# Down products of the feed-forward layers as seven products in two sweeps, with weight sums made by accumulating transfers

## The chip, the cores and the metric

One core of one Trainium2 chip runs the whole program. The metric is the device time of one execution in microseconds, the median of several runs.

## The reference

A stack of three layers over x of 512 tokens by 1024, all float32. Two layers (layer 0 and layer 1) have attention, a memory attention over 256 further tokens, and a gated feed-forward part; the last layer has two other attentions and a feed-forward part with squared relu. The change touches the last product of each feed-forward part:

```python
# layers 0 and 1, D_FF = 2816
h = rms_norm(x, norm_ffn_pre[i])
gu = jnp.einsum('bsd,df->bsf', h, w_gu[i])
f = jnp.einsum('bsf,fd->bsd', jax.nn.silu(gu[..., :D_FF]) * gu[..., D_FF:], w_down[i])
x = x + rms_norm(f, norm_ffn_post[i])
# last layer, D_FF_2 = 4096
a = relu(rmsnorm(x, norm_mlp_g) @ w_mlp_in) ** 2
x = x + a @ w_mlp_out
return rmsnorm(x, norm_final_g)
```

The last three lines are the reference's, in short. In the down product a 512 x 2816 (or 4096) matrix of activations meets a weight matrix of 2816 (4096) x 1024.

## The kernel before

Every float32 product is made of three float32r products: each factor is split into a high and a low part, and `mm3` (L262 to L264) issues high·high, high·low and low·high into one PSUM bank. The high part of a weight half chunk is an ACT cast (L250), the low part a DVE subtraction (L252); both stand in `split`. `loader` walks the list `order` and streams weight chunks of 512 KB (128 x 1024) with SP transfers (L236).

The order of the instructions is set when the program is built: tasks written as generators yield operations, and a list scheduler with priorities, tile pools ("slot", 37 tiles of 4 KB per partition, with a cap per use in `CAPS`) and a pool of 8 PSUM banks puts them one after another on each engine. On the chip each engine then runs its list in order and waits on semaphores.

A feed-forward part is `ffn` (L1354). Its up and gate products are already in a seven-product form: `seven` (matmuls L1224 to L1226 into `z`, column sums of weights on DVE at L1164, splits at L1090 and L1092). They leave activations in tiles `act`, features on partitions, two feature tiles of 128 x 512 tokens in each slot.

The down product is plain. A task in `ffn` splits every activation tile into `jit` tiles (ACT L1400, DVE L1402), once for each half of the output's 1024 columns. `out_product` (L491) takes the two halves in turn: four banks `acc`, one for each block of 128 tokens, over all 22 (32) feature tiles, three 128x512 matmuls each. So there are 2 x 4 x 22 x 3 = 528 matmuls in layers 0 and 1 each, and 768 in the last. In the second half of the columns the last 8 feature tiles are held back and done one token block after another, so that the blocks finish one by one.

The end of a block is `first_half` (L552: times the gain, or L545: into x) and `second_half` (L578 times the gain, L567 in the last layer; sum of squares on ACT at L406; `rsqrt` in eight small DVE steps L381 to L396; x plus the scaled product at L587). Then `to_norm` norms x for the next layer (L451), transposes it on PE (L465, tiles `ht`) and splits it (ACT L476, DVE L478) into the tiles `h` that the next projection reads.

In layer 0 the task of the second layer's memory keys and values is spawned from `post`, at the start of the down product: 96 matmuls 128x256 (`b<-mh,w` and `b<-w,mh`, through L262 to L264), with their own norm and transposes, then L642 and L644. In the order PE has most of them among the transposes of the tail.

Of the kernel before, what the change touches and what calls it, by code (L numbers as in the profile page):

```python
# [11 lines left out]
F32R = mybir.dt.float32r  # L12
# [7 lines left out]
S = 512  # L20
# [9 lines left out]
CAPS = dict(raw=2, w=8, q=2, k=4, p=5, pT=3, h=3, gain=2, f0=2, tmp=3, act=16, jit=8, bias=4, y=2,  # L30
# [125 lines left out]
class Chunk:  # L156


    def __init__(self, name, i):
        self.name, self.i = name, i  # L160
        self.half = [Fut(), Fut()]
        self.raw, self.unread = None, 2


class Builder:
# [9 lines left out]
    def setup(self):  # L175
# [22 lines left out]
        self.order = []  # L198
        self.hready = None
# [25 lines left out]
    def chunk(self, name, i):  # L225
        c = Chunk(name, i)
        self.order.append(c)
        return c

    def loader(self):  # L230
        nc, sc = self.nc, self.S
        for n, c in enumerate(self.order):
            r = yield ("get", "slot", "raw", 1)
            raw = self.tile_slot((P, 2, 512), name="raw")
            fin = yield ("op", "SP", r, 0.06)
            nc.sync.dma_start(raw.rearrange("p a b -> p (a b)"), self.ap[c.name][c.i])  # L236
            busy = self.arrival(fin, 512)
# [7 lines left out]
    def split(self, c, h, raw, ready, rel):  # L245
        nc, sc = self.nc, self.S
        r = yield ("get", "slot", "w", 1)
# [847 lines left out]
    def token_sums(self, out):  # L1095
# [14 lines left out]
        def put(name, src, t, dst=None):  # L1110
            if dst is None:
# [3 lines left out]
                self.held += 2  # L1115
# [64 lines left out]
    def seven(self, cs, gated, acts, slots, j0):  # L1180
# [11 lines left out]
        self.h_read, self.held = Fut(), 0  # L1192
# [10 lines left out]
        def product(n, name, banks, first=False, last=False, ready=0.0, waits=(None, None)):  # L1203
# [7 lines left out]
            for e in range(2):  # L1211
# [17 lines left out]
                if name in after:  # L1229
                    after[name](state[n], e, t)  # L1230
            return ts
# [75 lines left out]
        for n in range(nd):  # L1307
# [7 lines left out]
            s["rt"] = yield ("get", "slot", "tmp", 2)  # L1315
            s["ta"], s["tb"] = [self.tile_slot((P, 2, S), name="tmp") for _ in range(2)]
# [23 lines left out]
        sc.put("slot", sc.t["PE"], None, self.held)  # L1340
# [13 lines left out]
    def ffn(self, ci, co, nf, gated, post, nxt):  # L1354
# [35 lines left out]
        yield from self.seven(ci[4:], gated, acts, slots, 4 // per)  # L1390

        jit = {(k, half): Fut() for half in range(2) for k in range(nf)}

        def splitter(half):
            for k in range(nf):
                r = yield ("get", "slot", "jit", 1)
                w = self.tile_slot((P, 2, S), F32R, name="jit")
                f = yield ("fut", acts[k])
                t = yield ("op", "ACT", max(f.t, r), act(S, False))
                nc.scalar.copy(w[:, 0], f.val)  # L1400
                t = yield ("op", "DVE", t, dve(S))
                nc.vector.tensor_tensor(w[:, 1], f.val, _f(w[:, 0]), ALU.subtract)  # L1402
                reads[k // 2] += 1
# [600 lines left out]
```

## Time and profile before

| what | value |
|---|---|
| median of 3 runs | 1942.0 us (1941.7 to 1944.85) |
| profiled execution | 1943.43 us, span 1941.3 us, mean granted clock 0.995 |
| PE busy | 1903.5 us, 12282 instructions |
| DVE busy | 1351.7 us |
| ACT busy | 1012.2 us |
| POOL busy | 83.5 us |
| down products of layer 0 | 443.9 to 566.8 us, tail to 586.6 |
| down products of layer 1 | 1041.3 to 1162.2 us, tail to 1178.5 |
| down products of the last layer | 1759.3 to 1933.4 us, end at 1941.3 |

The span is the time from the first to the last recorded instruction of the profiled execution; its own time, 2.1 us longer, takes in what lies around. Busy time is a sum over instructions, so it says how full an engine is on average; what an engine waits for in one stretch is read from the rows of that stretch. Matmuls are pipelined: the time shown for one is longer than the distance from its start to that of the next.

### The profile page before, as it was taken

What the parts mean: (1) busy time and instruction counts of PE and PEld (TensorE: products, weight loads), DVE (VectorE), ACT (ScalarE), POOL (GpSimd) and SP (SyncE); (2) the same over time, 40 slices, a digit from 0 to 9 for tenths busy, and PEclk for the clock granted to TensorE, in tenths of its full rate; (3) what the DMA queues carried; (4) which work ended last, traced back from release to release, by engine and by line L of the source; (5) the groups of instructions that cost most, each with busy time, mean ns of one, the idle gap of its engine ahead of it and who ended that gap; (6) DMA issues with size and microseconds to landing.
All of it is one profiled execution on the core that took longest, in us unless ns stands there. A gap on an engine that the chain in (4) does not pass through costs nothing.

```text
span 1941.3 us, 31689 instructions
## 1 busy us (share of the span) xinstructions
PE 1903.5 (98%) x12282; PEld 1656.7 (85%) x12282; DVE 1351.7 (70%) x2767; ACT 1012.2 (52%) x2229; POOL 83.5 (4%) x145
## 2 busy tenths in 40 slices
PE   7999999999999999999999999999999999999998
PEld 6877899998887777899999889777778889998886
DVE  7576898887666665798888556337752659996562
ACT  6686455556545554455556535445553335555460
POOL 2000000000003221000000000000000000000000
PEclk9999999999999999999999999999999999999999
DMA  8113232332332333223323332231232322332331
GB/s 289 36 64 120 77 109 88 108 119 106 121 110 80 96 97 112 88 77 104 115 87 109 111 116 73 93 98 55 82 114 77 122 73 77 99 105 103 109 108 44
DMA packets 54149, 192.66 MB, mean 99 GB/s; under 512 B 6954, under 2 KB 6974, under 8 KB 54000
## 3 DMA queue, kind: packets, MB, share of 16 engines
q1 hardware_dynamic: 47664, 171.46, 26.3%
q0 software_dynamic: 6336, 19.19, 3.5%
q8 instruction: 96, 1.57, 0.3%
q14 instruction: 53, 0.43, 0.1%
HBM read 180.83 MB, written 3.17 MB: 95 GB/s over the span
## 4 chain that ended last, share of the span: by engine, by line
PE 94%; DVE 4%; ACT 1%; issue 1%; DMA 0%; SPq 0%; DVEq 0%; ACTq 0%
PE b L262 10%; PE acc L262 10%; PE acc L264 9%; PE acc L263 9%; PE b L264 9%; PE b L263 9%; PE z L1226 9%; PE z L1224 9%; PE z L1225 9%; PE o L709 3%; PE tr L682 3%; PE s L658 2%; PE s L661 2%; PE ht L465 1%; DVE w L1092 1%
## 5 line engine op out<-in xcount | busy, mean ns | idle before, releaser
L252 DVE TENSOR_TENSOR w<-raw,w 128x512 fp32r<-128x512 f32 x408 | 269.7, 688 | 133.9 <-ACT w L250 131.8
L1092 DVE TENSOR_TENSOR w<-raw,w 128x512 fp32r<-128x512 f32 x378 | 246.7, 688 | 36.8 <-ACT w L1090 34.6
L262 PE MATMUL b<-h,w 128*128 128x512 f32 (+1 forms) x736 | 269.4, 366 | 1.7 <-ACT h L476 1.7
L250 ACT CAST w<-raw 128x512 fp32r<-128x512 f32 x408 | 239.6, 620 | 32.5 <-DVE jit L1402 11.0
L263 PE MATMUL b<-h,w 128*128 128x512 f32 (+1 forms) x736 | 254.3, 346 | 1.4 <-DVE h L478 1.4
L264 PE MATMUL b<-h,w 128*128 128x512 f32 (+1 forms) x736 | 254.8, 346 | 0.0
L1090 ACT CAST w<-raw 128x512 fp32r<-128x512 f32 x378 | 223.6, 621 | 51.3 <-DVE raw L1164 50.7
L1226 PE MATMUL z<-h,w 128*128 128x256 f32 x864 | 242.4, 281 | 5.6 <-DVE w L1092 5.6
L1224 PE MATMUL z<-h,w 128*128 128x256 f32 x864 | 242.7, 281 | 1.0 <-ACT w L1090 1.0
L1225 PE MATMUL z<-h,w 128*128 128x256 f32 x864 | 241.6, 280 | 0.0
L262 PE MATMUL acc<-w,jit 128*128 128x512 f32 x608 | 237.4, 390 | 0.0
L264 PE MATMUL acc<-w,jit 128*128 128x512 f32 x608 | 236.7, 389 | 0.0
L263 PE MATMUL acc<-w,jit 128*128 128x512 f32 x608 | 236.5, 389 | 0.0
L1226 PE MATMUL z<-so,w 128*128 128x256 f32 x648 | 183.7, 284 | 3.0 <-DVE w L1092 2.9
L1224 PE MATMUL z<-so,w 128*128 128x256 f32 x648 | 183.5, 283 | 0.0
L1225 PE MATMUL z<-so,w 128*128 128x256 f32 x648 | 183.3, 283 | 0.0
L1226 PEld LDWEIGHTS z<-h,w 128*128 128x128 f32 x864 | 163.0, 189 | 6.7 <-DVE w L1092 6.7
L1224 PEld LDWEIGHTS z<-h,w 128*128 128x128 f32 x864 | 162.9, 188 | 1.4 <-ACT w L1090 1.4
L262 PEld LDWEIGHTS b<-h,w 128*128 128x128 f32 x736 | 139.1, 189 | 28.2 <-issue 10.3
L1225 PEld LDWEIGHTS z<-h,w 128*128 128x128 f32 x864 | 162.4, 188 | 0.0
L264 PEld LDWEIGHTS b<-h,w 128*128 128x128 f32 x736 | 139.2, 189 | 18.1
L1402 DVE TENSOR_TENSOR jit<-act,jit 128x512 fp32r<-128x512 f32 x152 | 103.3, 689 | 72.1 <-ACT jit L1400 71.5
(208 smaller groups left out, 3823.9 us busy)
## 6 DMA issues: line engine op xcount, KB each, us to landing
raw<-in_w_gu_dram SPq DMA_DIRECT2D x88, 512.0 KB, 3.9
raw<-in_w_in_dram SPq DMA_DIRECT2D x46, 512.0 KB, 3.5
raw<-in_w_down_dram SPq DMA_DIRECT2D x44, 512.0 KB, 3.4
raw<-in_w_mlp_in_dram SPq DMA_DIRECT2D x32, 512.0 KB, 4.1
raw<-in_w_mlp_out_dram SPq DMA_DIRECT2D x32, 512.0 KB, 3.2
raw<-in_w_out_dram SPq DMA_DIRECT2D x24, 512.0 KB, 3.2
raw<-in_w_in_b_dram SPq DMA_DIRECT2D x20, 512.0 KB, 3.8
raw<-in_w_in_a_dram SPq DMA_DIRECT2D x12, 512.0 KB, 8.4
```

The lines of the kernel that those rows point to most:

```text
L250: nc.scalar.copy(w[:, 0], raw[:, h])
L252: nc.vector.tensor_tensor(w[:, 1], raw[:, h], _f(w[:, 0]), ALU.subtract)
L262: nc.tensor.matmul(out, ah, bh, start=first, stop=False)
L263: nc.tensor.matmul(out, ah, bl, start=False, stop=False)
L264: nc.tensor.matmul(out, al, bh, start=False, stop=last)
L682: nc.tensor.transpose(bk[:m, o:o + P], p[:, j, k0:k0 + m], self.ident)
L1090: self.nc.scalar.copy(hi, src)
L1092: self.nc.vector.tensor_tensor(lo, src, _f(hi), ALU.subtract)
L1224: nc.tensor.matmul(o, wh, xh, start=first and clear and k == 0, stop=False, **g)
L1225: nc.tensor.matmul(o, wh, xl, start=False, stop=False, **g)
L1226: nc.tensor.matmul(o, wl, xh, start=False, stop=last and k == 3, **g)
L1402: nc.vector.tensor_tensor(w[:, 1], f.val, _f(w[:, 0]), ALU.subtract)
```

## The change

The down product becomes a seven-product form. Let A be the activations: A11 and A12 for tokens 256 to 511, A21 and A22 for tokens 0 to 255, the second index for the first or the second half of a unit's feature tiles. Let B be the weights: first index the half of the feature tiles, second the half of the 1024 columns. With s1 = A21 - A22, s2 = A11 - s1, s3 = A22 - s2, s4 = A12 - s2, and T1 = B11 + B12, T2 = T1 + B22, T4 = T2 + B21, T3 = B22 + B12, four products are summed over all features in a first sweep, and three in a second:

```diff
+    FIRST = (("A11", "B11"), ("s1", "T1"), ("s2", "T2"), ("A22", "T4"))
+    LATER = (("A12", "B21"), ("s4", "B22"), ("s3", "T3"))
...
+        def factor(u, b, e, r, w, free):
+            f = yield ("fut", wsrc[u, b, e])
+            src = f.val[:, e]
+            t = yield ("op", "ACT", max(r, f.t), act(512, False))
+            nc.scalar.copy(w[:, 0], src)
+            t = yield ("op", "DVE", t, dve(512))
+            tt(w[:, 1], src, _f(w[:, 0]), ALU.subtract)
+            wf[u, b, e].set(t, (w, free))
+            step = {"B11": ("T1", "B12"), "T1": ("T2", "B22"), "T2": ("T4", "B21"), "B22": ("T3", "B12")}
+            if b in step and "p" + step[b][0] not in units[u]:
+                yield from more(u, e, *step[b], f.val, t)
...
+        def more(u, e, b, add, raw, ready):
+
+            i, cs = units[u][add]
+            fin = yield ("op", "POOL", ready, 1.04)
+            nc.gpsimd.dma_start(raw[:, e], self.ap[name][i][:, cs[0] + 512 * e:cs[0] + 512 * e + 512],
+                                accum_op=ALU.add)
...
+            sums = {"s1": ("A21", "A21", "A22", ()), "s2": ("A21", "A11", "A21", ("s1",)),
+                    "s3": ("A22", "A22", "A21", ("s2", "A22")), "s4": ("A21", "A12", "A21", ("s3",))}
...
+                t = yield ("op", "DVE", t, dve(256 * ne))
+                tt(src, view(u, sums[a][1]), view(u, sums[a][2]), ALU.subtract)
+            t = yield ("op", "ACT", t, act(256 * ne, False))
+            nc.scalar.copy(hi, src)
+            t = yield ("op", "DVE", t, dve(256 * ne))
+            tt(lo, src, _f(hi), ALU.subtract)
```

A unit `u` is four feature tiles; layers 0 and 1 have six units (the first of half size), the last layer eight. Units go in groups of two. For each unit one piece of B11 is loaded by SP (L247), and T1, T2 and T4 are made from it in place, one after another: a DMA issued from POOL (`more`, L1452) adds the next part of the weights to the piece in SBUF as soon as the previous factor has been split (ACT L1438, DVE L1440). The second sweep loads B21 and B22 and makes T3 the same way. 44, 44 and 64 such transfers of 256 KB are issued. Some of the split weights lie in tiles of `h`, which the up products no longer read. The activation factors are split at L1523 (ACT) and L1525 (DVE), their differences made at L1521 (DVE).

After the first sweep four evacuations in two banks each (ACT L1584, DVE L1592) leave the parts that the blocks of the output share. The second sweep's last group of three units is taken one token block after another:

```diff
+            for i in range(2):
+                for u in g:
+                    t = yield from mms(u, "s3", "T3", bank["T3"], (i,), 0.0, False, u == g[-1])
+                both = [Fut(), Fut()]
+                for half in range(2):
+                    sc.spawn(piece(i, half, "T3", t, 0.1 * i, both[half]), 0.1 * i)
+                sc.spawn(self.when(both, lambda t: sc.put("bank", t)), 0.1 * i)
+            for i in range(2):
+                for half in range(2):
+                    a, b = self.LATER[half]
+                    for u in g:
+                        t = yield from mms(u, a, b, bank[b], (i,), 0.0, False, u == g[-1])
+                    sc.spawn(piece(2 + i, half, b, t, 0.1 * (2 + i)), 0.1 * (2 + i))
...
+        def piece(tb, half, b, t, prio, free=None):
...
+            t = yield ("op", "DVE", max(t, f.t), dve(512))
+            tt(out, src[:, i], ps, ALU.subtract if (tb < 2 and half == 0) else ALU.add)
+            free.set(t) if free else sc.put("bank", t)
+            fs = Fut()
+            sc.spawn(self.sum_task(out, ss[tb][:, half:half + 1], t, fs), prio)
+            g = yield ("fut", post)
+            yield ("fut", fs)
+            t = yield ("op", "DVE", max(t, g.t), dve(512))
+            tt(out, out, g.val[:, 512 * half:512 * half + 512], ALU.mult)
```

So a block needs, for each half of its columns, one combination of bank and stored part (L1658), one multiplication by the gain (L1665) and one addition to x (L1682); in the last layer the stored parts are added to x earlier (L1601) and the end is one operation for each half (L1642). Layer 1's memory task is spawned at the start of the second sweep (`between`), and weight chunks of the next layer are split only once all down factors are (`c.after`):

```diff
+        def late():
+            co["go"].set(0.0)
+            self.down_factors(co, slots, acts)
+        yield from self.seven(ci[4:], gated, acts, slots, 4 // per, late)
+
+        yield from self.down_seven(co, post, nxt, between)
...
-            def post(i=i):
+
+            def between(i=i):
                 if i == 0:
                     sc.cap["gain"] = 3
                     sc.spawn(self.memory[1][0](1.6), 1.6)
-                return self.load_gain("norm_ffn_post", i)
```

In the changed program lines lie a little lower: `mm3` is L275 to L277, the weight split L263 and L265, the norm L464, the transposes L478 and the h split L491.

How the order moves. First PE at the end of layer 0's down product. Before, the last `acc` matmul is followed by four transposes of h (`ht<-ident,h`), then memory products (`b<-mh,w`):

```order
L263 MATMUL acc<-w,jit 128x512
L264 MATMUL acc<-w,jit 128x512
L465 MATMUL ht<-ident,h 128x128 x4
L262 MATMUL b<-mh,w 128x256
L263 MATMUL b<-mh,w 128x256
L264 MATMUL b<-mh,w 128x256
L262 MATMUL b<-mh,w 128x256
```

So memory products start after one token block's first transposes. At a later place of the same tail, before, the last memory products, the last transposes and layer 1's first projection (`b<-h`) follow one another:

```order
L262 MATMUL b<-w,mh 128x256
L263 MATMUL b<-w,mh 128x256
L264 MATMUL b<-w,mh 128x256
L465 MATMUL ht<-ident,h 128x128 x8
L262 MATMUL b<-h_71,w 128x512
L263 MATMUL b<-h_73,w 128x512
```

All 96 memory matmuls thus lie ahead of the last transposes. In the change the first of these places reads:

```order
L275 MATMUL acc<-w,jit 128x512
L276 MATMUL acc<-w,jit 128x512
L277 MATMUL acc<-w,jit 128x512
L478 MATMUL ht<-ident,h 128x128 x28
L275 MATMUL b<-mh,w 128x256
L276 MATMUL b<-mh,w 128x256
L277 MATMUL b<-mh,w 128x256
L478 MATMUL ht<-ident,h 128x128 x4
L275 MATMUL b<-mh,w 128x256
L276 MATMUL b<-mh,w 128x256
```

Four transposes have become 28 in a row, with one memory product of three matmuls before the last four; the other 93 memory matmuls stand behind those, and the first projection behind them.

Next, PE at the end of layer 1, in the change (`b<-h` is the last layer's first projection):

```order
L276 MATMUL acc<-w,jit 128x512
L277 MATMUL acc<-w,jit 128x512
L478 MATMUL ht<-ident,h 128x128 x24
L275 MATMUL b<-h_71,w 128x256
L276 MATMUL b<-h_73,w 128x256
L277 MATMUL b<-h_71,w 128x256
```

The 24 transposes stand together. Nine matmuls further on:

```order
L276 MATMUL b<-h_73,w 128x256
L277 MATMUL b<-h_71,w 128x256
L478 MATMUL ht<-ident,h 128x128 x8
L275 MATMUL b<-h_71,w 128x256
L276 MATMUL b<-h_73,w 128x256
```

There are twelve projection matmuls between 24 transposes and the last eight; before, the first eight transposes were followed by projection matmuls, and the others came among these.

DVE, from the first closing operation of layer 0 on, in the change:

```order
L1658 TENSOR_TENSOR f_5675<-f_5675,acc 128x512
L1658 TENSOR_TENSOR y<-f_5674,acc 128x512
L1665 TENSOR_TENSOR f_5675<-f_5675,gain 128x512
L1521 TENSOR_TENSOR act<-act 128x2x256
L1665 TENSOR_TENSOR y<-y,gain 128x512
L1440 TENSOR_TENSOR w<-raw,w 128x512
L1525 TENSOR_TENSOR jit<-act,jit 128x512
L1521 TENSOR_TENSOR act<-act 128x2x256
L1440 TENSOR_TENSOR w<-raw,w 128x512 x2
L1525 TENSOR_TENSOR jit<-act,jit 128x512
L1440 TENSOR_TENSOR w<-raw,w 128x512 x8
```

The closings of the first block stand ahead of eleven further weight splits (`w<-raw`) and of the rsqrt steps; before, DVE had weight splits only ahead of its first closing operation, and then closing work alone up to the last h splits.

POOL in the change, layer 0's down product (`raw<-in_w_down_dram` is the accumulating transfer):

```order
L215 DMA gain<-in_norm_mix_post_dram 128x1024
L215 DMA gain<-in_norm_ffn_pre_dram 128x1024
L1452 DMA raw<-in_w_down_dram 128x512 x34
L215 DMA gain<-in_norm_ffn_post_dram 128x1024
L215 DMA gain<-in_norm_mix_pre_dram 128x1024
L1452 DMA raw<-in_w_down_dram 128x512 x10
L215 DMA k<-k 64x256 x4
```

The 44 accumulating transfers stand between loads of gains and ahead of the key copies of layer 1.

## Rows read from the trace of the kernel before

**Rows 1.** The page, busy time, share of the span and instructions of each engine

```profile
PE 1903.5 (98%) x12282; PEld 1656.7 (85%) x12282; DVE 1351.7 (70%) x2767; ACT 1012.2 (52%) x2229; POOL 83.5 (4%) x145
```

**Rows 2.** The page, chain of work that ended last, share by engine

```profile
PE 94%; DVE 4%; ACT 1%; issue 1%; DMA 0%; SPq 0%; DVEq 0%; ACTq 0%
```

**Rows 3.** Stretches: length, busy us (count) of engines, granted clock, DMA share, GB/s

```profile
443.90:566.80 122.90, 122.88 (x555) 101.33 (x553) 82.23 (x170) 65.88 (x126) 0.00 (x0) 1.00 0.27 91
566.80:586.60 19.80, 15.86 (x121) 14.40 (x121) 17.58 (x46) 11.71 (x23) 4.13 (x8) 0.95 0.53 173
586.60:591.70 5.10, 5.06 (x12) 4.00 (x13) 5.10 (x8) 2.81 (x6) 5.10 (x3) 0.51 0.00 0
1041.30:1162.20 120.90, 120.90 (x540) 100.03 (x540) 74.33 (x148) 59.17 (x114) 0.00 (x0) 1.00 0.27 88
1162.20:1178.50 16.30, 15.34 (x129) 14.71 (x128) 15.27 (x44) 8.47 (x20) 0.53 (x1) 1.00 0.51 193
1759.30:1933.40 174.10, 174.10 (x769) 143.91 (x768) 93.42 (x162) 73.35 (x134) 0.00 (x0) 1.00 0.25 83
1933.40:1941.30 7.90, 0.11 (x1) 0.00 (x0) 3.53 (x11) 0.72 (x2) 0.00 (x0) 0.69 0.27 104
```

**Rows 4.** Timeline of PE, down products of layer 0: start, us, line, tile

```profile
539.14 0.39 PE L262 MATMUL acc<-w,jit 128*128 128x512 f32 x1
...
539.82 0.39 PE L262 MATMUL acc<-w,jit 128*128 128x512 f32 x1
```

**Rows 5.** Timeline of PE, end of layer 0's tail and start of layer 1

```profile
583.66 1.48 PE L465 MATMUL ht<-ident,h 128*128 128x128 f32 x8 [2.98 <-DVE h L451]
...
586.64 0.79 PE L263 MATMUL b<-h,w 128*128 128x512 f32 x1 [0.35 <-DVE h L478]
587.23 0.63 PE L264 MATMUL b<-h,w 128*128 128x512 f32 x1
587.66 0.63 PE L262 MATMUL b<-h,w 128*128 128x512 f32 x1
```

**Rows 6.** Timeline of DVE, down stage of layer 0 and its tail

```profile
462.93 1.89 DVE L1402 TENSOR_TENSOR jit<-act,jit 128x512 fp32r<-128x512 f32 x3
464.74 0.68 DVE L252 TENSOR_TENSOR w<-raw,w 128x512 fp32r<-128x512 f32 x1
...
550.26 0.69 DVE L578 TENSOR_TENSOR y<-acc,gain 128x512 f32<-128x512 f32 x1 [7.53 <-ACT junk L406]
...
552.65 0.75 DVE L587 SCALAR_TENSOR_TENSOR x<-f,rs,x 128x512 f32<-128x512 f32 x1
553.32 0.75 DVE L587 SCALAR_TENSOR_TENSOR x<-y,rs,x 128x512 f32<-128x512 f32 x1
...
557.34 0.15 DVE L392 SCALAR_TENSOR_TENSOR rs<-rs 128x1 f32<-128x1 f32 x1
557.46 0.16 DVE L390 SCALAR_TENSOR_TENSOR rs<-rs 128x1 f32<-128x1 f32 x1
...
585.48 2.13 DVE L478 TENSOR_TENSOR h<-ht,h 128x512 fp32r<-128x512 f32 x2 [0.61 <-ACT h L476]
```

**Rows 7.** Groups of DVE in 443.9 to 586.6: busy, mean ns | idle before

```profile
L252 DVE TENSOR_TENSOR w<-raw,w 128x512 fp32r<-128x512 f32 x46 | 31.6, 689 | 8.1 <-ACT w L250 7.8
L1402 DVE TENSOR_TENSOR jit<-act,jit 128x512 fp32r<-128x512 f32 x43 | 29.2, 689 | 17.8 <-ACT jit L1400 17.7
```

**Rows 8.** Timeline of DVE, last h split in the tail of layer 1

```profile
1177.67 0.69 DVE L478 TENSOR_TENSOR h<-ht,h 128x512 fp32r<-128x512 f32 x1
```

**Rows 9.** DMA queues: packets, MB, share of 16 engines

```profile
q1 hardware_dynamic: 47664, 171.46, 26.3%
q0 software_dynamic: 6336, 19.19, 3.5%
```

**Rows 10.** DMA issues: count, KB each, median us to landing

```profile
vs<-vb POOLq DMA_DIRECT2D x3, 256.0 KB, 3.1
```

**Rows 11.** Groups of POOL: busy, mean ns | idle before

```profile
L214 POOL DMA_DIRECT2D vs<-vb x6 | 3.1, 528 | 22.2 <-ACT vb L363 22.2
```

More of the change, by code (lines that the diff above doesn't have):

```diff
@@ L198, in setup @@
         self.order = []
+        self.after = None
         self.hready = None
@@ L225, in chunk, with piece @@
     def chunk(self, name, i):
-        c = Chunk(name, i)
+        c = Chunk(name, i, self.after)
+        self.order.append(c)
+        return c
+    def piece(self, name, i, cols, go):
+        c = Chunk(name, i, go, cols)
+        c.raw, c.piece = Fut(), True
         self.order.append(c)
@@ L246, in split @@
         nc, sc = self.nc, self.S
+        if c.after is not None:
+            yield ("fut", c.after)
         r = yield ("get", "slot", "w", 1)
@@ L1178, in column_sums, with seven @@
                     yield from one(i, name)
-    def seven(self, cs, gated, acts, slots, j0):
+    def seven(self, cs, gated, acts, slots, j0, late):
         nc, sc = self.nc, self.S
@@ L1230, in product @@
                     after[name](state[n], e, t)
+            if n == nd - 1 and name in ("T1", "T2", "T3"):
+                sc.put("slot", t, None, 2)
+                if name == "T1" and not gated:
+                    late()
             return ts
@@ L1315, in seven @@
             s["rt"] = yield ("get", "slot", "tmp", 2)
+            if n == nd - 1 and gated:
+                late()
             s["ta"], s["tb"] = [self.tile_slot((P, 2, S), name="tmp") for _ in range(2)]
@@ L1355, in ffn @@
+    def ffn(self, ci, co, nf, gated, post, nxt, between):
         nc, sc = self.nc, self.S
@@ L1389, in ffn @@
             sc.spawn(evac(j, first[j * per:(j + 1) * per]), 1 + 0.01 * j)
[L1390 to L1403, printed above, removed]
-                if reads[k // 2] == 4:
-                    sc.put("slot", t)
-                jit[k, half].set(t, (w[:, 0], w[:, 1], lambda z: sc.put("slot", z, "jit")))
-        def splits():
-            yield from splitter(0)
-            yield from splitter(1)
-        sc.spawn(splits(), 1.4)
-        yield from self.out_product(co, nf, lambda k, half: jit[k, half], post(), nxt())
+        def late():
[3 more added lines that the diff above has]
+        yield from self.down_seven(co, post, nxt, between)
     def dil_order(self, d):
@@ L1751, in plan @@
             p["gu"] = [c(f"w_gu{i}", j) for j in range(2 * D_FF // P)]
-            p["down"] = [c(f"w_down{i}", j) for j in range(D_FF // P)]
+            p["down"] = self.down_plan(f"w_down{i}", D_FF // P)
             pl.append(p)
```

297 lines of the change are left out of this document (283 added, 14 removed).

## The prediction

> **What bounds the kernel now.** I read the page's busy line first, then its chain, then the stages. TensorE (PE) is busy 98% of the span [rows 1], and the chain that ended last lies on it for 94%, with VectorE (DVE) at 4% [rows 2]. The table by stretch shows where that holds [rows 3]: in the three down stages (443.9 to 566.8, 1041.3 to 1162.2, 1759.3 to 1933.4 us) PE is busy for the whole of 122.9, 120.9 and 174.1 us at a granted clock of 1.00, while DVE has 82.2, 74.3 and 93.4 us of work and the DMA engines are used to 0.25 to 0.27. So in those stretches time is matmuls times their spacing. From 539.14 to 539.82 are three starts of 128x512 matmuls [rows 4]: 0.227 us each (the 0.39 in the row is the time from start to modelled end). Behind each down stage stands a tail on DVE: sums of squares, rsqrt, residual, norm, split of the transposed h. In layer 0 it ends with the split that starts at 585.48, and the last transposes wait 2.98 us on DVE [rows 5, 6].
>
> All sums here are made against the profiled execution, 1943.43 us (span 1941.3); the runs' median is 1.4 us under it.
>
> **Matmuls removed.** By the order, down products fall from 528 + 528 + 768 to 462 + 462 + 672: 228 fewer, all 128x512. By 0.227 us that is 51.7 us: 15.0, 15.0 and 21.8. This is the whole gain to be had.
>
> **Work added to DVE in the sweeps.** A wide DVE operation back to back costs 0.60 us (from 462.93 to 464.74 are three, [rows 6]). Before, the layer 0 stretch up to 586.6 holds 46 weight splits and 43 factor splits [rows 7]. By the order of the change, DVE executes between the last up/gate sum and the first closing operation of layer 0 118 wide operations (59 weight splits, 32 factor splits, 17 factor differences, 6 evacuations, 4 others), 7 half ones and some small: 118 x 0.60 + 7 x 0.33 + 5 = 78 us. PE needs for the 372 matmuls up to there 84.3 us plus 2 us of transposes. Layer 1: 130 wide, 80 us, against 84.3. Last layer: about 210 wide and 10 of the three-operand kind, 139 us, against 672 x 0.227 = 152.3. In all three DVE stays under PE, by 4 to 13 us, and the order puts the splits 6 to 20 us ahead of their matmuls, so I cost the sweeps at nothing beyond PE. The cover is thin: if ACT or a transfer holds DVE up, these few us are gone and DVE sets the pace. ScalarE (ACT) does one cast per split at about the same length without the differences, and is freer still.
>
> **Tail of layer 0.** Here the cover ends. The seven-product form closes all four token blocks near the end, whereas before half the columns (first half) were closed long before and only the second half was left. From the first closing operation to the last h split the order gives DVE 34 wide operations (20.4 us), 16 of the three-operand kind at 0.67 (552.65 to 553.32, [rows 6]; 10.7 us), 64 small rsqrt steps at 0.13 where two chains interleave (557.34 to 557.46; 8.3 us) and 9 h or mh splits at 1.1 or 0.6 (9.5 us): 49 us. Before, the same chain from the first L578 at 550.26 to 587.6 took 37.3 us, of which some 4 to 5 idle in waits between ACT and DVE; I add 4. The first T3 product is ready 86.3 us after the start, so the last h split ends at 86.3 + 49 + 4 = 139 us. PE stopped with its last product at 86.3 + 90 x 0.227 = 107 and stands with few transposes to do. Worse, the order puts 93 of the memory products of the next layer (256 wide) behind the last transposes, where before they filled the gaps between them. By 15.34 us for 129 instructions [rows 3] these take 0.119 each, 11 us; they begin with the last transposes, some 4 us before that split ends. Layer 1 then begins 139 - 4 + 11 = 146 us after the start. Before it was 586.64 - 443.9 = 142.7. **Layer 0: +3, against -15.0 by matmuls alone.** Bounds: if the tail is as well packed as the order allows and PE's products come early, -6; if each block pays a wait, +10.
>
> A clock drop comes with it: after the wait at 583.66 the granted clock was 0.51 for 586.6 to 591.7 [rows 3], matmuls started 0.43 apart in place of 0.227 [rows 5], 2.4 us lost. That level (1.2 GHz) followed a stretch in which PE waited; it will come again after the idle tail, in layer 0 on the memory products (no change), in layer 1 newly (+2.4).
>
> **Tail of layer 1.** DVE: 18 wide, 16 three-operand, 64 small, 8 h splits at 0.61: 34.6 us, plus 4 idle, after a first T3 product at 84.3: 123 us. The order has 24 transposes, 12 products, 8 transposes, then the bulk of the next projection, which so begins at 123 - 1.4 + 2.4 = 124. Before, h was finished at 1178.4 [rows 8] but 117 of the next products had been done between 1162.2 and 1178.5 (13.8 us): equivalent to a start at 123.4. **Layer 1: about 0, against -15.0**; bounds -8 and +6.
>
> **Last layer.** No gain multiplication, and the blocks' sums into x lie before the end. DVE is under PE; after the last product one block is to be closed, as now (the 7.9 us from 1933.4, [rows 3]). **-21.8, of which I give back 4** for the first group, whose T1, T2, T4 are made one out of another: each step is an issue, a landing and a split, against 5.44 us of PE per product (24 x 0.227). Bounds -21.8 and -10.
>
> **The accumulating transfers.** 152 new ones of 256 KB, from POOL. No such transfer is in the trace. Nearest rows: plain loads took 26.3% of 1941.3 us for 171.46 MB, so 0.78 us of all engines per 256 KB; the software queue 3.5% for 19.19 MB, 0.93 us [rows 9]. A 256 KB software transfer lands in 3.1 us [rows 10], an issue holds POOL 0.53 us [rows 11]. POOL has nothing else to do there but gain loads. Lower bound 0.78 us, upper bound 3.1 us (one after another, with nothing overlapped). Per half feature unit the first sweep needs one load and three of these, and PE takes 4 x 6 x 0.227 = 5.44 us: it is hidden up to (5.44 - 0.78) / 3 = 1.55 us. I take 0.93, the queue's own row: 3.6 us against 5.44, hidden. Four pieces (two units each way) are in flight, so landing may take some 10 us before it shows, outside of the first group.
>
> The Trainium skill, "Collectives: The Full Stack", section "The bandwidth ceiling: the fold count and why AG ≠ RS ≠ AR", says a reducing transfer reads two sources and so runs at half the rate of a copy. By it the price would double; no run here shows it, and the sum above is by the copy's row.
>
> **Sum:** +3 + 0 - 17.8 = -15 on the profiled execution, 1928.4; less 1.4 for the median: **1927 us**.
>
> **Rivals.**
> (1) *The tails are hidden*: DVE's closing work slips between splits, and PE's saving stays whole: 1942 - 51.7 = 1890; with a few us of waits 1890 to 1903. For it: DVE has idle time before its tail, and the order interleaves. Against it: 49 us of DVE behind a product ready at 86 us is more than PE has left (20 us).
> (2) *The accumulating transfers set the pace* (slower). If one takes two passes of the engines, 2 x 0.93 = 1.86 us, a half unit takes 0.78 + 3 x 1.86 = 6.36 us against 5.44; 38 half units lose 0.92 each, 35 us, some 10 of it covered by the pieces loaded ahead: 1927 + 25 = 1952. At the upper bound of 3.1 it is 10.1 against 5.44, +176 us, about 2100. It decides from 1.55 us: from there matmuls wait for splits that wait for transfers. For it: reading the destination as well is more work than any copy in the trace. Against it: DMA stands at a quarter [rows 3], and most of the landing time is latency that overlaps. The Trainium skill's rule just cited gives this case.
> (3) *DVE and ACT, now at 90% and more of PE in layers 0 and 1, pace the sweeps*: every late landing stops ACT's and DVE's queues, since they run in order, and the tails start later by what is lost: +5 in each layer and in the last: 1938 to 1946, no change.
> That the change does not do what it says can be left out: the order shows the 228 matmuls gone.
>
> **Chances.** Forecast 0.50 (1916 to 1938), rival 1 0.12, rival 2 0.20, rival 3 0.18, of which a third ends faster, a third at no change, a third slower. A measurement here tells about 0.2%, 3.9 us. Faster: 0.50 + 0.12 + 0.06 = 0.68; same: 0.06 of rival 3 and 0.04 for the mild end of rival 2, 0.10; slower: 0.06 + 0.16 = 0.22. The range leaves out rival 1's better half and the costly half of rival 2: 1902 to 1956.
>
> **What would show it.** Right: acc matmuls still 0.227 apart in the sweeps, PE idle between the last acc of layers 0 and 1 and the last transposes, waiting on DVE's L464 and L491; layer 1 starting about 146 us after 443.9. Rival 1: no such idle time. Rival 2: acc matmuls waiting for splits (L1440), these for ACT's L1438, these for DMA, with 256 KB landing in well over 4 us and the software queue's share above 1.55 us for each. Rival 3: DVE without gaps while PE waits within the sweeps. The forecast is wrong if PE's waits inside the sweeps exceed 10 us, or those of the tails fall under 10.

## The result, and the profile after

The changed kernel takes **2006.71 us** (median of 4 runs) against 1942.63: ratio 1.032, interval 1.030 to 1.034. The forecast was 1927, range 1902 to 1956. It is slower by 64 us, and outside the range, on the side of rival 2.

The page of the changed kernel: busy time by engine, DMA queues (packets, MB, share of 16 engines), the chain, DMA issues (count, KB each, median us to landing):

```profile
PE 1885.9 (94%) x12054; PEld 1625.8 (81%) x12054; DVE 1475.7 (74%) x2991; ACT 1065.6 (53%) x2337; POOL 210.5 (11%) x297
...
q1 hardware_dynamic: 47520, 168.84, 25.1%
q0 software_dynamic: 28224, 59.04, 15.4%
...
PE 30%; DMA 5%; DVE 4%; ACT 2%; issue 1%; POOL 0%; DVEq 0%; ACTq 0%; POOLq 0%
...
raw<-in_w_down_dram POOLq DMA_DIRECT2D x88, 256.0 KB, 6.3
...
raw<-in_w_mlp_out_dram POOLq DMA_DIRECT2D x64, 256.0 KB, 7.4
```

228 matmuls are gone, as forecast, and PE's busy time falls by only 17.6 us [rows 1], since part of the rest ran at the lower clock (the mean granted clock is 0.975, before 0.995). The software queue went from 3.5% of 1941.3 us [rows 9] to 15.4% of 2004.8: 67.9 to 308.7 us of all 16 engines. If the queue's other transfers took what they took before, that is 240.8 / 152 = **1.58 us for each accumulating transfer** of 256 KB, and it lands in 6.3 to 7.4 us.

DMA, nothing in the chain before [rows 2], holds 5% of the span in it, about 100 us. The shares of this row add up to 42%, because the chain could be followed back only to 1157.8 us, in layer 1; 94 of the 100 us stand in the last layer's down product. The chain of that stretch, before (1759 to 1934) and in the change (1813.9 to 1995.5):

```profile
by line: PE acc L264 33.2%; PE acc L262 33.2%; PE acc L263 33.1%; DVE x L567 0.4%; PE z L1226 0.1%; PE z L1224 0.1%; PE z L1225 0.1%; issue 0.0%
by line: DMA raw<-in_w_mlp_out_dram 51.6%; issue 7.4%; PE acc L276 5.3%; PE acc L277 5.0%; PE acc L275 4.9%; DVE h L1440 4.8%; DVE jit L1525 3.5%; POOL raw L1452 3.2%; ACT w L1438 3.0%; ACT h L1438 2.6%; DVE act L1521 2.5%; DVE w L1440 2.4%
```

So in a stage whose chain was matmuls, half of the chain is now landings, the time from the issue of a transfer to its arrival.

Stretches of the changed kernel (length, busy us of PE, PEld, DVE, ACT, POOL, granted clock, DMA share, GB/s): first sweep, second sweep and tail of layer 0; both sweeps of layer 1; both sweeps and the end of the last layer:

```profile
444.70:510.50 65.80, 63.74 (x266) 49.95 (x266) 47.65 (x80) 37.23 (x70) 25.09 (x30) 0.97 0.96 203
510.50:573.90 63.40, 49.94 (x216) 39.30 (x214) 54.33 (x120) 36.04 (x75) 8.73 (x10) 0.92 0.62 166
573.90:613.10 39.20, 20.00 (x130) 18.57 (x129) 33.94 (x85) 18.95 (x35) 3.22 (x6) 0.70 0.30 94
1066.10:1132.50 66.40, 63.49 (x266) 50.10 (x265) 47.48 (x80) 37.00 (x70) 25.41 (x31) 0.97 0.95 200
1132.50:1193.50 61.00, 49.58 (x200) 38.69 (x198) 48.55 (x97) 31.31 (x63) 8.59 (x11) 0.92 0.58 161
1813.90:1911.10 97.20, 92.13 (x387) 71.26 (x386) 71.24 (x114) 54.61 (x98) 37.45 (x44) 1.00 0.89 179
1911.10:1995.40 84.30, 70.77 (x289) 54.72 (x287) 66.65 (x120) 39.54 (x76) 12.65 (x15) 0.94 0.53 141
1995.50:2004.80 9.30, 0.27 (x2) 0.00 (x0) 5.45 (x20) 0.72 (x2) 0.00 (x0) 0.70 0.30 113
```

Against [rows 3], the DMA share in the first sweeps is 0.89 to 0.96 where it was a quarter. Products alone would take 264 x 0.227 = 59.9 us in the first sweep of layers 0 and 1, 87.2 in the last layer; the stretches are 6, 7 and 10 us longer. The larger loss is in the second sweeps, where DMA is at 0.53 to 0.62: 198 (288) products would take 44.9 (65.4) us, and with 1.4 us of transposes in layer 0 the loss is 17, 16 and 19 us.

What PE waited for in the whole changed kernel (us in total, times, longest), and the wait in layer 0's second sweep:

```profile
PE ht L478 <- DVE h L464: 42.6, 9, 9.0
PE acc L276 <- DVE h L1440: 17.3, 12, 10.9
PE acc L275 <- ACT h L1438: 14.3, 6, 8.1
PE acc L276 <- DVE w L1440: 13.4, 11, 8.3
```

```profile
527.44 0.40 PE L275 MATMUL acc<-h,jit 128*128 128x512 f32 x1
538.71 0.80 PE L276 MATMUL acc<-h,jit 128*128 128x512 f32 x1 [10.88 <-DVE h L1440]
```

The first line, by stretch (layer 0's tail, layer 1's tail, the first 20 us of the kernel):

```profile
PE ht L478 <- DVE h L464: 19.2, 4, 5.8
PE ht L478 <- DVE h L464: 10.6, 3, 4.0
PE ht L478 <- DVE h L464: 12.8, 2, 9.0
```

So 29.8 us of it are the tails, and the rest stands at the start of the kernel, as before (13.0 us there). The other three lines, 45 us, are factors that came late: DVE's and ACT's splits there wait for DMA. In layer 0's second sweep POOL, ACT and DVE read:

```profile
520.39 7.88 POOL L1452 DMA_DIRECT2D raw<-in_w_down_dram  x9 [10.23 <-ACT junk L419]
...
532.41 0.62 ACT L1438 CAST w<-raw 128x512 fp32r<-128x512 f32 x1 [3.42 <-DMA raw<-in_w_down_dram]
...
533.06 0.69 DVE L1440 TENSOR_TENSOR w<-raw,w 128x512 fp32r<-128x512 f32 x1 [2.75 <-ACT w L1438]
...
537.98 0.68 DVE L1440 TENSOR_TENSOR h<-raw,h 128x512 fp32r<-128x512 f32 x1
```

Nine additions are issued in a row and land one after another, from 3.7 to 14.7 us after their issue. The product that PE waits for is, by the order of the products, one of B22, which SP loads and no addition makes. Its split stands in DVE's queue (537.98) behind five splits of factors that additions make, each waiting for a landing. Layer 1's longest wait, 8.3 us, is of the same kind. In the last layer PE waits 8.1 us for a T3; that wait is read with the runs below.

In starts of matmuls (the copies are a run below; a tail is taken to the first `b<-h` product in layer 0 and to the first `b<-w,h` product in layer 1; the last row runs to the end of the span):

| part | before | changed | with copies |
|---|---|---|---|
| layer 0, first to last down product | 122.4 | 129.0 | 112.0 |
| layer 0, tail | 19.1 | 39.4 | 39.9 |
| layer 1, first to last down product | 120.4 | 127.2 | 110.4 |
| layer 1, tail | 27.1 | 47.2 | 46.3 |
| last layer, first up product to first down product | 143.2 | 148.4 | 148.3 |
| last layer, first to last down product | 173.9 | 181.5 | 155.7 |
| last layer, from there to the end | 8.2 | 9.4 | 9.4 |

The row of the up products is a loss ahead of the sweeps, and copies keep it. PE's waits there, before and in the change:

```profile
PE z L1226 <- DVE w L1092: 2.3, 3, 1.5
PE z L1238 <- DVE w L1105: 5.3, 3, 4.6
```

Four splits of the first down factors (L1440) stand in DVE's queue ahead of the last three splits of up weights (L1105, at 1804.46). PE waits 4.56 us for these, and the clock granted behind it is 0.50 (1805.6 to 1808.6).

### The profile page after: what moved, and what is told of

Its sections match the earlier page's. It is cut to its first block, busy times and chain, and to the rows that moved or that the text cites. A ratio compares the mean times of both kernels' runs of the same rounds, so it can differ in the third digit from the quotient of the medians.

```text
span 2004.8 us, 32041 instructions
## 1 busy us (share of the span) xinstructions
PE 1885.9 (94%) x12054; PEld 1625.8 (81%) x12054; DVE 1475.7 (74%) x2991; ACT 1065.6 (53%) x2337; POOL 210.5 (11%) x297
## 3 DMA queue, kind: packets, MB, share of 16 engines
q0 software_dynamic: 28224, 59.04, 15.4%
## 5 line engine op out<-in xcount | busy, mean ns | idle before, releaser
L1105 DVE TENSOR_TENSOR w<-raw,w 128x512 fp32r<-128x512 f32 x378 | 246.8, 688 | 34.6 <-ACT w L1103 32.5
L275 PE MATMUL b<-h,w 128*128 128x512 f32 (+1 forms) x736 | 268.3, 365 | 0.9 <-ACT h L489 0.9
L277 PE MATMUL b<-h,w 128*128 128x512 f32 (+1 forms) x736 | 254.1, 345 | 4.0 <-DVE w L265 4.0
L265 DVE TENSOR_TENSOR w<-raw,w 128x512 fp32r<-128x512 f32 x256 | 166.3, 693 | 121.2 <-ACT w L263 120.5
L1103 ACT CAST w<-raw 128x512 fp32r<-128x512 f32 x378 | 223.9, 621 | 47.1 <-DVE raw L1176 45.1
L1238 PEld LDWEIGHTS z<-h,w 128*128 128x128 f32 x864 | 165.1, 191 | 9.7 <-DVE w L1105 9.7
L1236 PEld LDWEIGHTS z<-h,w 128*128 128x128 f32 x864 | 165.1, 191 | 1.4 <-ACT w L1103 1.4
L1237 PEld LDWEIGHTS z<-h,w 128*128 128x128 f32 x864 | 164.6, 191 | 0.0
L275 PEld LDWEIGHTS b<-h,w 128*128 128x128 f32 x736 | 138.9, 189 | 26.5 <-issue 10.5
L277 PEld LDWEIGHTS b<-h,w 128*128 128x128 f32 x736 | 138.7, 188 | 22.5 <-DVE w L265 4.5
L276 PEld LDWEIGHTS b<-h,w 128*128 128x128 f32 x736 | 139.4, 189 | 12.8 <-DVE h L491 1.1
L1452 POOL DMA_DIRECT2D raw<-in_w_down_dram x88 | 75.8, 1090 | 698.7 <-DMA raw<-in_w_down_dram 566.0
L263 ACT CAST w<-raw 128x512 fp32r<-128x512 f32 x256 | 144.7, 620 | 2.7 <-DMA raw<-in_w_mem_kv_dram 2.4
L1176 DVE TENSOR_TENSOR raw<-raw 128x512 f32<-128x512 f32 x216 | 142.7, 686 | 0.0
L276 PE MATMUL acc<-w,jit 128*128 128x512 f32 x308 | 122.7, 398 | 13.8 <-DVE w L1440 13.4
```

What stands on the lines that cost most here:

```text
L263: nc.scalar.copy(w[:, 0], raw[:, h])
L265: nc.vector.tensor_tensor(w[:, 1], raw[:, h], _f(w[:, 0]), ALU.subtract)
L275: nc.tensor.matmul(out, ah, bh, start=first, stop=False)
L276: nc.tensor.matmul(out, ah, bl, start=False, stop=False)
L277: nc.tensor.matmul(out, al, bh, start=False, stop=last)
L1103: self.nc.scalar.copy(hi, src)
```

## The experiments

All but the last two of these were executed once. Executions of one kernel lie some us apart: ten of one of them went from 1943 to 1951 us, and the kernel before gave 1943.5, 1939.5, 1940.4 and 1940.5 beside the four sets of single runs. So each is read against the kernel before of its own set, and a difference under some 8 us rests on the stages in the trace, not on the time alone.

**Copies in place of additions, all layers** (the sums of weights are left out):

```diff
-            nc.gpsimd.dma_start(raw[:, e], self.ap[name][i][:, cs[0] + 512 * e:cs[0] + 512 * e + 512],
-                                accum_op=ALU.add)
+            nc.gpsimd.dma_start(raw[:, e], self.ap[name][i][:, cs[0] + 512 * e:cs[0] + 512 * e + 512])
```

> The 152 transfers from POOL copy instead of adding, so the sums of weights are left out; every instruction, its place in its queue and every byte to SBUF stay. Theory A (an accumulating transfer holds the 16 DMA engines for about 1.6 us per 256 KB, twice a copy, and this paces the sweeps): the software queue's share falls from 15.4% to about 10%, landing from 6 to 7 us to about 3.5, the 462 products of layer 0 take 107 us instead of 129, and the time falls to 1930 to 1945. Theory B (the order of the queues: each factor waits for issue, landing and split of the one before, whatever the transfer costs): 1985 or more. Theory C (DVE paces the sweeps): 1995 or more.

Measured: **1946.8** beside 1943.5. 60 us come back. The queue's row on the page, and the two stretches of layer 0's sweeps:

```profile
q0 software_dynamic: 18496, 59.04, 9.8%
```

```profile
444.10:504.50 60.40, 60.40 (x267) 49.52 (x266) 52.12 (x89) 40.34 (x76) 16.12 (x30) 1.00 0.73 239
504.50:556.40 51.90, 49.57 (x216) 39.57 (x214) 48.42 (x111) 32.64 (x69) 5.33 (x10) 0.97 0.51 177
```

A copy takes (190.6 - 67.9) / 152 = 0.81 us of the engines, and lands in 4.0. So the addition costs 1.95 copies. It also has more packets, 28224 against 18496 for the same 59.04 MB: 144 for each addition and 80 for each copy. In the trace those with data carry 2 KB in an addition and 4 KB in a copy, and both take 0.19 to 0.20 us. Plain 2 KB packets of SP's queue take 0.09, so smaller packets alone are not the reason. With copies PE never waits in layer 0's first sweep. Theory A holds, though the time is a little over its 1945 and layer 0's products take 112, not 107 us; the other two fall: the orders alone, and DVE with the same instructions in the same queues, hold PE up by one wait of 2.2 us in layer 0's sweeps. The chain of the last layer's down product has 8.5% of landings in place of 51.6%. This run shortens both, engine time and landing, and so does not part them.

**Half the bytes** (the other half of each sum is left out):

```diff
-            nc.gpsimd.dma_start(raw[:, e], self.ap[name][i][:, cs[0] + 512 * e:cs[0] + 512 * e + 512],
+            nc.gpsimd.dma_start(raw[:, e, :256], self.ap[name][i][:, cs[0] + 512 * e:cs[0] + 512 * e + 256],
                                 accum_op=ALU.add)
```

> The accumulating transfers add only the first 256 of each 512 columns, so half of each sum of weights is left out: as many transfers, rows and issues, half the bytes. If the cost goes with the bytes, 0.8 us each and 1930 to 1950; if it goes with the number of rows, 1.6 us as before and about 2000. Theory B: 1985 or more.

Measured: 1954.6 beside 1943.5. The page's row:

```profile
q0 software_dynamic: 28224, 39.12, 10.7%
```

As many packets as in the changed kernel, and (209.0 - 67.9) / 152 = 0.93 us each: mostly bytes (1.58 to 0.93 for half of them), with a part that stays. The time is 5 us over the range expected for bytes, 8 above the copies. The landing falls too, to a median of 4.4 us over the three layers (6.9 in the changed kernel), so this run does not part the two either.

**Only the last layer in the new form.** Layers 0 and 1 get the two-half product of before again:

```diff
+        if gated:
...
+            between()
+            yield from self.out_product(co, nf, lambda k, half: jit[k, half], post(), nxt())
+            return
```

> Layers 0 and 1 have their down products as before, only the last layer has the seven products with accumulating transfers. If the layers' losses are independent, what the changed kernel lost in layers 0 and 1 (27 us each) goes and the last layer's 8 us stay: about 1950. If what layers 0 and 1 do spoils the last layer's start too: under 1942.

> As the run with only the last layer, with copies in place of the additions there, so the sums of weights are left out. Theory A: the last layer keeps nearly its 21.8 us, 1920 to 1928. Theory B or C: 1945 or more.

Measured: 1957.2 and 1924.8, beside 1943.5. With additions the last layer alone makes the kernel 13.8 us slower, not some 7 as expected (1950), since the 5 us of the up products come on top. With copies the kernel is 18.7 us faster. Of these the last layer itself gives 14: its down products take 153.7 us (20.2 less), its up products 148.4 (5.2 more), its end 9.1 (0.9 more). The other 4 to 5 us lie in the layers ahead of it, where the program is the one of before: its first up product starts at 1611.8 us, before at 1616.1. Where the additions hurt, POOL and then PE in the last layer of the first of these two:

```profile
1893.85 0.84 POOL L1452 DMA_DIRECT2D raw<-in_w_mlp_out_dram  x1 [15.63 <-DVE h L1440]
1895.05 0.83 POOL L1452 DMA_DIRECT2D raw<-in_w_mlp_out_dram  x1 [0.36 <-issue]
1896.26 6.09 POOL L1452 DMA_DIRECT2D raw<-in_w_mlp_out_dram  x7 [0.37 <-issue]
1903.12 0.84 POOL L1452 DMA_DIRECT2D raw<-in_w_mlp_out_dram  x1 [0.77 <-DMA raw<-in_w_mlp_out_dram]
```

```profile
1907.62 0.40 PE L277 MATMUL acc<-h,jit 128*128 128x512 f32 x1
1916.12 0.80 PE L275 MATMUL acc<-h,jit 128*128 128x512 f32 x1 [8.11 <-ACT h L1438]
```

POOL's queue stands 15.6 us at one T3 addition whose B22 split is late, and then issues nine and, at 1903.12, a tenth. Where nothing else is under way they land 1.28 us apart, the tenth at 1915.43. That one makes the factor for which PE starves 8.1 us, and PE comes back at the lower clock (granted 0.50). By the order of the products it is a T3 of the group before the last. Six of the additions ahead of it belong to the last group: its T3 has a load of B22 of its own, so it waits for no split (as T1 of the first group has one of B11), and it is wanted later. So the addition that PE needs first stands last in POOL's queue.

With copies POOL has the same ten in a row:

```profile
1868.33 0.54 POOL L1452 DMA_DIRECT2D raw<-in_w_mlp_out_dram  x1 [10.86 <-DVE h L1440]
...
1870.73 3.72 POOL L1452 DMA_DIRECT2D raw<-in_w_mlp_out_dram  x7 [0.66 <-PE acc L277]
```

They land 0.65 us apart where nothing else is under way, half the distance of the additions, and PE does not wait. The burst thus comes from the fixed order; what an addition costs decides whether PE feels it.

**Some of the sums on GpSimd, last layer only.** SP loads the part to be added, GpSimd adds:

```diff
+            if (u, b) in parts:
+                f = yield ("fut", parts[u, b])
+                w = f.val[0]
+                t = yield ("op", "POOL", max(ready, f.t), 1.75)
+                nc.gpsimd.tensor_tensor(raw[:, e], raw[:, e], w[:, e], ALU.add)
```

> As the run with only the last layer, but 12 of the 64 additions there (T1 of every group but the first) are made by GpSimd from a part loaded by SP, and 52 stay accumulating transfers. Theory A: engine time per half unit of the first sweep falls from 0.78 + 3 x 1.58 = 5.5 us to 2 x 0.78 + 2 x 1.58 = 4.7, against 5.44 us of products, so most of the first sweep's waits go and part of those at the end: 1940 to 1950 instead of 1957. Theory B (queue order): 1957 or more, since POOL now also holds additions of some 1.7 us (twice the 0.84 us of a 128x248 one) in its queue.

> As the run before, T3 too by GpSimd where it is made from a split B22 (so 12 and 10 of the 64). Theory A: 5 us better again, 1935 to 1947, because the second sweep's transfers fall as well. Theory B: no better than with T1 alone.

> T1 and T2 by GpSimd (12 and 16 of the 64), T4 and T3 by accumulating transfers. Theory A: the transfers of the first sweep take 3 x 0.78 + 1.58 = 3.9 us per half unit and GpSimd 2 x 1.7 + 0.85 = 4.3 us, both under 5.44: 1930 to 1940. If GpSimd's additions hold up DVE, DVE's wide operations get longer than 0.60 us apart and the time stays over 1950.

Measured: 1959.1, 1954.9 and 1959.3, beside 1939.5: no gain, so theory A fails in all three. From its first up product to the end the last layer takes 341, 338 and 342 us, with all sums by transfer 338. Groups of DVE in the last layer (busy, mean ns), with all sums by transfer (first), and with T1 and T2 on GpSimd, with GpSimd's own (second):

```profile
L1440 DVE TENSOR_TENSOR w<-raw,w 128x512 fp32r<-128x512 f32 x48 | 32.2, 687 | 11.5 <-ACT w L1438 11.2
```

```profile
L1440 DVE TENSOR_TENSOR w<-raw,w 128x512 fp32r<-128x512 f32 x46 | 39.0, 865 | 3.1 <-ACT w L1438 3.1
...
L1465 POOL TENSOR_TENSOR raw<-raw,part 128x512 f32<-128x512 f32 x28 | 51.7, 1860 | 30.7 <-DVE w L1440 17.6 <-DVE h L1440 13.1
```

While GpSimd adds, DVE's split goes from 687 to 865 ns in the mean: 684 where no addition of GpSimd overlaps it, 1235 in the 15 where one does. DVE is then busy for 163.5 of the 184.3 us of down products, with all sums by transfer for 137.9 of 180.5, so most of the cover is used up. The burst of T3 stays as well: PE's longest wait there is 8.0 us. The Trainium skill ("GPSIMD Engine Reference", section "1. Specifications") says that GpSimd shares its SBUF interfaces with VectorE, with contention where a DVE instruction has two SBUF inputs; the trace agrees, with these 178 ns.

**The tail without the gain** (copies in all layers; the multiplication by the gain before the residual of layers 0 and 1 is left out):

```diff
-            t = yield ("op", "DVE", max(t, g.t), dve(512))
-            tt(out, out, g.val[:, 512 * half:512 * half + 512], ALU.mult)
```

> As the run with copies in all layers, and the multiplication by the gain before the residual is left out in layers 0 and 1 (16 wide DVE operations, 4.8 us in each tail). If DVE's chain sets the tails, each of the two layers gets 4 to 5 us shorter: 1937 to 1940 instead of 1946.8. If PE's transposes or ACT set them, under 2 us in all.

Measured: 1934.9 beside 1939.5, 4.6 under, where the copies with the gain were 3.4 over: 8 us for 16 operations of 0.60 (9.6). Layer 0's tail falls from 39.9 to 36.0, layer 1's from 46.3 to 40.9, the 4 to 5 us expected in each. DVE's chain sets the tails.

**The planner's cost of an addition, and more pieces in flight**:

```diff
-            t = self.arrival(fin, 256) + 0.5
+            t = self.arrival(fin, 512) + 2.0
```

```diff
-                sc.cap["piece"] = 6
+                sc.cap["piece"] = 10
```

> As the run with only the last layer, with one change in the planner's costs: an accumulating transfer counts with 512 KB and 2.0 us more (before: 256 KB and 0.5 us), so the fixed orders of ACT and DVE are laid out for the landing that was measured. If the waits come from orders made for a cheap transfer, part of the 13.8 us of that run comes back: 1945 to 1950. If the engines' time itself sets the pace, within 3 us of it.

> As the run with only the last layer, but in the second sweep up to ten pieces of weights may be in flight instead of six. If the last group's T3 waits because its pieces are loaded late, the burst of ten additions before it spreads and PE's wait of 8 us there goes: 1945 to 1950. If free tiles, not the cap, hold the loads, no change.

> Both edits together in the last layer: 1940 to 1947 if the order is what is left of the loss beside the first sweep's 5 us, 1954 or more if it is the engines' time.

> The changed kernel with the planner's cost of an accumulating transfer raised in all three layers. If orders made for a cheap transfer cost much of the 60 us that the copies gave back, 1975 to 1990; if the engines' time does, 2000 or more.

Measured, beside 1940.4: 1949.5 with the cost, 1941.7 with the pieces, 1950.1 with both, and **1974.9** with the cost in all three layers. So orders that count with a late landing get back about 30 of the changed kernel's 64 us (in layer 0 the down products take 122.0 in place of 129.0, in layer 1 114.2 for 127.2, in the last 174.1 for 181.5). The transfers themselves cost what they cost before: 15.4% of 1973.1 us, 1.55 us each, and they land in 6.7 to 7.2 us. In the last layer alone the same edit gives about 5, too little for one run to tell (its down products take 176.3 for 180.5), and the pieces 12 (9 when timed, below). Both together lie between the two values expected, so the two do not add up and this run decides nothing.

> The changed kernel in all three layers with ten pieces in flight in the second sweep. If the loads that come late in the second sweep are most of the 60 us, 1965 to 1980; if free tiles hold the loads in layers 0 and 1, where the act tiles are fewer, only the last layer gains: 1990 to 1995.

Measured: 2009.7 beside 1940.5, a miss. The last layer's down products do get 8 us shorter (173.2 from 181.5), but those of layers 0 and 1 do not (131.0 and 127.3), and layer 0's tail grows to 51 us from 39.4. There the new order has put more work on DVE, which sets the tail: 113 operations, 41.6 us, in place of 85 and 34.0.

**Versions that might beat both**, from the last layer alone with ten pieces:

> As the run with only the last layer and ten pieces in flight, and the last group of the second sweep does B21 and B22 before T3, so that T3, which is made by the late burst of additions, is wanted 16 us later. If PE's wait before the last group (5 us there) is the burst, it goes: 1934 to 1938, under the kernel before. If the engines' time is the limit there, no change: 1941 or more.

> As the first of this set, with up to six pieces in the first sweep too, instead of four. If the first sweep's 5 us are landing time, 2 to 4 us better than that run; if they are the engines' time, no change.

> As the first of this set, with the planner counting an accumulating transfer as 384 KB and 1.0 us. If ACT and DVE orders still wait on landings, up to 3 us better; if not, within 2 us either way.

Measured beside 1940.5: 1946.5 with the tail in another order, 1951.1 with six pieces in the first sweep as well, 1950.6 with a middle cost. The last two have the other tail order too. None gains, against an expected 1934 to 1938 for the first. PE's wait before the last group, 3.8 to 4.5 us with ten pieces alone, is 0.9 in the first of them, and a wait of 1.65 us elsewhere took part of its place. Last, over five rounds:

> As the run with only the last layer and ten pieces in flight, but the 16 sums T3 of the second sweep are added by DVE from parts that SP loads, so only the 48 additions of the first sweep stay accumulating transfers. If the wait before the last group (5 us) and the smaller ones in the second sweep are the burst of T3 transfers, they go and 16 x 0.6 us of DVE stay hidden: 1934 to 1938, a little under the kernel before. If DVE has no room there: 1942 or more.

> The run with only the last layer and ten pieces in flight again, timed over five rounds. The single look gave 1941.7 beside 1940.4: no change against the kernel before, within 0.2%.

Measured: 1949.3 with T3 on DVE (ratio 1.0037, interval 1.0024 to 1.0049), 1947.05 with ten pieces (1.0024, interval 1.0013 to 1.0036), beside 1942.73. Both are slower by little, 0.37% and 0.24%, and in both the interval stays above 1. In the first, DVE has no idle time in which the sums could lie (start, us; it is busy for all of 1890 to 1904):

```profile
1896.57 1.28 DVE L1465 TENSOR_TENSOR raw<-raw,part 128x512 f32<-128x512 f32 x2
1897.77 0.68 DVE L1547 TENSOR_TENSOR jit<-act,jit 128x512 fp32r<-128x512 f32 x1
1898.45 1.29 DVE L1440 TENSOR_TENSOR w<-raw,w 128x512 fp32r<-128x512 f32 x2
1899.67 1.89 DVE L1465 TENSOR_TENSOR raw<-raw,part 128x512 f32<-128x512 f32 x3
```

and PE waits there 6.3 us for a split, in place of the burst. No version tried with additions by transfer is under the kernel before. With ten pieces the last layer's down products alone are shorter than before, 169.5 and 172.7 us against 173.9; the up products ahead of them, 147.7 against 143.2, and the end take that back.

## Why the prediction was wrong

The forecast was 1927. With copies the kernel takes 1946.8, so of the 80 us that it is over the forecast 60 are the additions', and 20 are there without them.

- **Matmuls removed, 51.7 us: right.** The order has them gone, and with copies the sweeps take 378.1 us against 416.7: 38.6 of it arrive, 18.2 in the last layer, and single waits with their clock drops and the transposes of layer 0 hold the rest. With additions the three stages together are 21 us longer than with 228 more matmuls.
- **"I take 0.93, the queue's own row: 3.6 us against 5.44, hidden": the step that failed.** An addition is 1.58 us of all engines, 1.95 times a copy here, and lies between the bounds named, at the 1.55 us that the text gave as the point of decision. The price was taken from the nearest row, a copy. But the price alone is not the error: put into the prediction's own comparison it gives 0.78 + 3 x 1.58 = 5.52 us against 5.44, 3 us over all 38 half units. The comparison of rates was the wrong measure, since it leaves the landing off the path. T1, T2, T4 and T3 are each an issue, a landing and a split in fixed queues; the landings are half of the chain in the last layer's down product (94 us), and PE waits 45 us for splits.
- **The cited rule.** The Trainium skill ("Collectives: The Full Stack", "The bandwidth ceiling: the fold count and why AG ≠ RS ≠ AR") states for the reduce step of a collective that it needs two source reads and gets half the rate of a copy. The trace has that ratio for an accumulating transfer within one core, 1.58 against 0.81 us; that the second read is the reason is not shown.
- **Rival 2 named the mechanism and mis-sized it.** Its signs all came: matmuls waiting for L1440, these for L1438, these for DMA, landings of 6.3 to 7.4 us, 1.58 us each. It gave 1952 at 1.86 us each, by a rate for the first sweep alone. The first sweeps lost 6, 7 and 10 us. What it left out is the second sweep, with 17, 16 and 19 us at a mean DMA share of 0.53 to 0.62: in POOL's fixed queue the last T3 additions stand together, nine in layer 0 and ten in the last layer, and the splits that wait for them hold others back. An average share says nothing of a burst.
- **"I cost the sweeps at nothing beyond PE", because the order puts the splits 6 to 20 us ahead:** that lead holds only if a landing takes what the planner assumed. That "landing may take some 10 us before it shows" was wrong: it showed with medians of 6.3 to 7.4, and single landings took up to 14.7. When the planner counts with more, half of the 64 us go.
- **Tails of layers 0 and 1: right in kind and nearly in size.** Between the last down product and layer 1's first product 39 us were forecast and 39.4 measured, with PE waiting on L464 as said (29.8 us in the two tails, in seven waits). In layer 1, from the last down product to where the bulk would begin, 19 were forecast and 22 measured, 20 with copies. With copies layer 0 still ended 10 us later than before, not 3, and layer 1 9 later, not 0: the tails were nearly as forecast, but the sweeps ahead of them took 112.0 and 110.4 us, not 107 and 104.7. In each of them PE waits 2 to 3 us for splits, and some 2 us go at the lower clock behind these waits.
- **Last layer, -17.8: right in kind, and near in size in part by luck.** With copies in this layer alone the whole kernel is 18.7 us faster, but the layer itself only 14. The down products give 20.2 of the 21.8. The 4 us given back for the first group are lost, with one more, in the up products ahead, where DVE's queue has the first down factors; the prediction puts nothing there.
- **Rival 3** (DVE and ACT pace the sweeps) is excluded as the pace by the copies, which keep all of DVE's and ACT's work. Its premise, that a late landing stops their queues, is what the rows of layers 0 and 1 show.

What stays open: the 60 us are the additions', but they were not parted cleanly into engine time and landing. Both fall together when an addition becomes a copy. The planner's cost, which changes neither, gets back half, so that half is an order that does not fit the landing.

## What to carry to other kernels

Price a transfer that adds as two copies, in time of the engines, and count with a landing well over a copy's (6.3 to 7.4 us against 4.0 here) in any fixed order. Comparing mean rates is not enough where each step waits for the landing of the one before: follow the chain, and look in each in-order queue for what stands ahead of the item that is wanted first. Where no trace has such a transfer, let the range reach as far as that price, worked out for every stage it feeds, not only for the one with the most of them. A product form that saves matmuls pays in what it asks of DVE and DMA: here the closings of four blocks at once ate the saving of layers 0 and 1, and the sums of weights that of the last layer and more. And a stage half idle on average can still starve in one burst behind an in-order queue.

## What the runs showed of the hardware

- An accumulating transfer from POOL has 144 packets where a copy of the same 256 KB has 80, takes 1.58 against 0.81 us of the 16 engines, lands in 6.3 to 7.4 against 4.0 us, and holds POOL 0.85 us (median) for its issue against 0.54. In a burst additions land 1.28 us apart, copies 0.65. At half the bytes an addition takes 0.93 us.
- The data packets of an addition carry 2 KB and take 0.19 us in the mean; a copy's carry 4 KB and take 0.20, and plain 2 KB packets of SP's queue 0.09.
- GpSimd's additions of 128x512 take 1.6 us when few (12) and 1.86 to 2.06 when more of them (28 and 22) run beside DVE, whose two-input operations then go from 687 to 865 ns.
- After the 10.88 us wait of PE in layer 0 the granted clock is 0.50 and the products start 0.43 us apart for some 3 us, as after the shorter waits of the tails [rows 5].
